# A two-layer hybrid attention block on one core: earlier-free memory under two sets of loads, another weave of LayerNorm rows, four groups in the second down phase

## The chip, the core and the metric

One of the eight cores of a Trainium2 chip runs the whole program. The metric is the device time of one execution in microseconds (us), smaller is better, over repeated executions. The engines are named as in the profile: PE (TensorE matmul) with PEld (its weight loads), DVE (VectorE), ACT (ScalarE), POOL (GpSimd), SP (SyncE, which here only issues DMA transfers). SPq and POOLq are the sequencers of SP and POOL, which issue transfers in program order.

## The reference, cut to what matters

Two layers over 1024 latent tokens (and 256 context tokens in layer 0), model width 1024, all in float32:

```python
for i in range(2):
    y, yc = mixer_i(h, hc)                       # attention, then @ w_out
    x = layer_norm(ALPHA * x + g1 * y, ln1_g, ln1_b)
    h = x * (1.0 + sc2) + sh2
    x = layer_norm(ALPHA * x + g2 * conv_ffn(h, w_up, conv_w, conv_b, w_down), ln2_g, ln2_b)
```

Layer 0 mixes by grouped-query and neighbourhood attention, layer 1 by multi-head latent attention (MLA, 16 heads). `conv_ffn` projects to 2 x 2816 features, convolves the gate half along the tokens, multiplies and projects back. In layer 0 the context tokens go through all of it too.

## The kernel before, in words

Every float32 product is made of three matmuls on split operands (`three`): a value is cast to a high part (`split_hi`, L404, mostly on ACT) and the rest goes to a low part (`split_lo`, L412, on DVE or POOL). So each block of weights and activations costs one cast and one subtraction before PE can use it.

The tokens stand in three chunks: 0 and 1 are 512 latent tokens each, 2 the 256 context tokens (layer 0 only). After attention, `layer_tail(l)` does the rest of a layer in these stages:

- **proj** (L1320 to L1341): y @ w_out in eight output blocks m, into `acc`. Layer 0 first reads y back from DRAM (`load_y`, L1288, tiles `yr`, stored as `y_scr` by the attention), and takes chunks 0 and 2 together, then chunk 1. `load_wo` (L1303) loads and splits one block of w_out (`ro`, then `foh`, `fol`). In layer 1 y is still in SBUF.
- **ln1 rows** (L1405): per 128 tokens a `normalise` (L1344: transposes `pta`, the sum `za`, its statistics), then eight `back_rows` (L1374: transposes `pba`, scaled into `tmpa`, split to `h`). For chunk 1 also 20 steps that make the operands P5, P6, P7, P4, P3. They are Python generators: each `next` emits a row, so the order of the calls sets the program order.
- **up phase** (`up_step`, L1459): products `pu` of a Strassen-Winograd scheme, seven products (P1 to P7) per pair of feature blocks, with weight conversions `wP` and, between, the convolution.
- **down phase** (`down_items`, `down_step`): the ten pairs of feature blocks are taken in `GROUPS` (L1612). A group passes all seven products; each product of a group writes four PSUM tiles (`pd_P`), and DVE adds each into its accumulators (`gated`, L1781, `acd<-pd_P`). The weights of a group are summed (L1208 to L1220) and split on DVE, POOL and ACT.
- the end of the layer: `last_down`, `ln2`, and after layer 0 `layer1_head` (w_in, rms, `rotate`, `up_kv`, `up_q`), which writes q, k, v of the MLA to DRAM. Then the first head is loaded (`prep1`, L2229, on POOL's queue) and attention of layer 1 runs.

Memory is in pools that share addresses over time: a tile may be written once the last users of what lay there are done, and the order in which tags are first used sets which addresses they get. `T` (`tail{l}`, tags c4, r, b) lies over memory of the attention before it; `AC` (`acc{l}`), `E` (`end{l}`), and the pools of the first head (`att1f`) lie over memory of the stage before. Outside attention a scheduler orders the instructions of each engine from the program order and the dependencies.

The caller, in short:

```python
for m in range(2):
    load_wo()
if l == 0:
    load_y(0); load_y(2); load_y(1)
run(proj((0, 2) if l == 0 else (0,)))
rows = itertools.chain(ln1(2), ln1(0)) if l == 0 else ln1(0)
for _ in proj((1,)):
    for _ in range(3 if l == 0 else 2):
        next(rows, None)
```

## Time and profile before

| | |
|---|---|
| median of 3 runs | 3521.74 us (3517.38 to 3532.01) |
| the profiled execution | 3522.96 us, span in the trace 3521.1 us |
| PE busy | 3291.1 us, 93% of the span |
| DVE, ACT, POOL busy | 70%, 50%, 42% of the span |
| mean granted clock of TensorE | 0.972 of full speed |
| layer 0's tail (proj to `layer1_head`) | about 807 to 2160 us |
| MLA attention | 2171 to 2701 us |
| layer 1's tail | 2704 to the end; its down phase 3249 to 3461 us |

A row of the timeline gives start, duration, engine, line, operation, output and inputs, and in brackets how long the engine was idle before it and what ended the idle time. Since PE is busy for all but some 230 us, the time of the kernel is read from the places where PE is idle or runs at a lower clock.

### The profile page before, as it was taken

How to read it: one execution, taken by the hardware profiler on the slowest of the kernel's cores; microseconds unless marked ns; L12 is line 12 of the kernel's file. 1: busy time of each engine (PE TensorE's matmuls, PEld its weight loads, DVE VectorE, ACT ScalarE, POOL GpSimd, SP SyncE). 2: the span in 40 equal slices, each digit the busy share in tenths (PEclk: the TensorE clock that was granted, in tenths of full speed). 3: DMA queues.
4: the chain of work that ended last, by engine and by line, in shares of the span. 5: the costliest groups of instructions: out<-in, count | busy, mean ns of one | idle time of the engine just before them, and what ended most of it. 6: DMA issues, size and time to landing. Idle time of an engine off the chain costs nothing.

```text
span 3521.1 us, 52490 instructions
## 1 busy us (share of the span) xinstructions
PE 3291.1 (93%) x18730; PEld 2834.5 (81%) x18730; DVE 2480.9 (70%) x3850; ACT 1755.3 (50%) x3335; POOL 1461.3 (42%) x1714
## 2 busy tenths in 40 slices
PE   7998899888889999999999998999999989999997
PEld 5987788877778888888877777999998768888786
DVE  6687687774698888686765534777776476777776
ACT  4222677774464444443335323777776354444342
POOL 4543688651200000035634522888885200000864
PEclk9999999999999999999999998999999999999998
DMA  6357511665345554263323457233333333334541
GB/s 217 114 186 223 134 44 31 159 182 166 126 154 156 168 169 157 76 230 120 99 65 102 132 211 228 50 83 76 72 77 88 117 105 102 111 99 144 191 135 72
DMA packets 385314, 455.05 MB, mean 129 GB/s; under 512 B 28500, under 2 KB 256764, under 8 KB 385052
## 3 DMA queue, kind: packets, MB, share of 16 engines
q1 hardware_dynamic: 371852, 425.08, 40.1%
q10 hardware_dynamic: 11424, 18.94, 1.5%
q0 software_dynamic: 1776, 7.67, 0.7%
q8 instruction: 148, 2.42, 0.3%
q14 instruction: 114, 0.93, 0.1%
HBM read 329.31 MB, written 122.22 MB: 128 GB/s over the span
## 4 chain that ended last, share of the span: by engine, by line
PE 42%; DVE 4%; POOL 3%; ACT 2%; issue 2%; DMA 2%; SPq 0%; POOLq 0%; ACTq 0%; DVEq 0%
PE pu L1459 10%; PE pd_P L1789 8%; PE psum L194 6%; PE psum L335 4%; PE psum L304 4%; PE pw L417 2%; PE psq L417 2%; PE pso L417 2%; PE px L1789 1%; PE pl L417 1%; PE psk L417 1%; PE psv L417 0%; POOL dr L1216 0%; DMA k<-kr_scr 0%; DMA dr<-in_l_w_down_dram 0%
## 5 line engine op out<-in xcount | busy, mean ns | idle before, releaser
L194 PE MATMUL psum<-k,q 96*128 96x512 f32 (+1 forms) x1152 | 273.1, 374 | 13.8 <-DMA k<-kr_scr 11.2
L412 POOL TENSOR_TENSOR dP<-dr,dP 128x512 fp32r<-128x512 f32 x40 | 56.1, 1421 | 487.6 <-ACT dP L404 465.1
L412 POOL TENSOR_TENSOR aal<-aa,aah 128x512 fp32r<-128x512 f32 x32 | 50.7, 1595 | 447.5 <-ACT aah L404 372.6
L194 PEld LDWEIGHTS psum<-k,q 96*128 96x128 f32 x1152 | 197.2, 193 | 42.4 <-issue 11.6
L264 POOL TENSOR_SCALAR p_m<-p_m,st_m 128x640 f32<-128x640 f32 x256 | 201.8, 801 | 12.6
L320 DVE TENSOR_TENSOR pl_m<-psum,ph_m 128x512 fp32r<-128x512 f32 x256 | 174.8, 684 | 37.4 <-ACT ph_m L314 36.4
L304 PE MATMUL psum<-ident,p_m 128*128 128x128 f32 x1280 | 193.3, 274 | 2.5 <-DVE pl_m L320 2.2
L251 ACT ACTIVATE p_m<-psum,st_m 128x1024 f32<-128x1024 f32 (+2 forms) x192 | 186.8, 983 | 17.0 <-DVE st_m L244 16.1
L314 ACT CAST ph_m<-psum 128x512 fp32r<-128x512 f32 x256 | 150.5, 589 | 88.7 <-PE psum L304 39.4
L552 DVE SCALAR_TENSOR_TENSOR aa<-aw,silu_late,aa 128x512 f32<-128x512 f32 x224 | 186.7, 862 | 8.1 <-DMA aw<-in_l_w_ada_dram 7.4
L335 PE MATMUL psum<-ph_m,v 128*128 128x256 f32 x640 | 175.3, 301 | 0.6 <-DVE y_m L353 0.6
L1781 DVE SCALAR_TENSOR_TENSOR acd<-pd_P,mods,acd 128x512 f32<-128x512 f32 x196 | 142.0, 742 | 44.8 <-PE pd_P L1789 44.6
L335 PE MATMUL psum<-ph,v 128*128 128x256 f32 (+1 forms) x512 | 150.4, 317 | 23.2 <-DVE y L368 12.1
L241 DVE TENSOR_REDUCE st_m<-psum 128x1 f32<-128x1024 f32 (+1 forms) x128 | 105.5, 824 | 88.1 <-PE psum L194 88.0
L320 DVE TENSOR_TENSOR pl<-psum,ph 128x512 fp32r<-128x512 f32 (+1 forms) x224 | 144.6, 647 | 31.1 <-ACT ph L314 28.0
L335 PE MATMUL psum<-pl_m,v 128*128 128x256 f32 x640 | 164.0, 282 | 0.0
L304 PE MATMUL psum<-ident,p 128*128 128x128 f32 x960 | 151.9, 278 | 10.4 <-ACT p_c L118 4.2
L264 POOL TENSOR_SCALAR p<-p,st 128x640 f32<-128x640 f32 x192 | 152.3, 801 | 12.6
L314 ACT CAST ph<-psum 128x512 fp32r<-128x512 f32 (+1 forms) x224 | 122.8, 557 | 67.5 <-PE psum L304 60.5
L304 PEld LDWEIGHTS psum<-ident,p_m 128*128 128x128 f32 x1280 | 149.0, 141 | 3.7 <-DVE pl_m L320 3.1
L304 PEld LDWEIGHTS psum<-ident,p 128*128 128x128 f32 x960 | 110.5, 142 | 28.9 <-DVE pl L320 8.2
L335 PE MATMUL psum<-pl,v 128*128 128x256 f32 (+1 forms) x512 | 132.5, 282 | 0.0
(605 smaller groups left out, 11283.4 us busy)
## 6 DMA issues: line engine op xcount, KB each, us to landing
aw<-in_l_w_ada_dram SPq DMA_DIRECT2D x96, 512.0 KB
ur<-in_l_w_up_dram SPq DMA_DIRECT2D x176, 256.0 KB
ar_P<-a_scr SPq DMA_DIRECT2D x140, 256.0 KB
a_scr<-a_t SPq DMA_DIRECT2D x80, 256.0 KB
dr<-in_l_w_down_dram SPq DMA_DIRECT2D x80, 256.0 KB
ro<-in_l_w_out_dram SPq DMA_DIRECT2D x64, 256.0 KB
a_scr<-cv SPq DMA_DIRECT2D x60, 256.0 KB
v<-v_scr SPq DMA_DIRECT2D x17, 640.0 KB
```

The costliest lines, as they stand in the source:

```text
L194: nc.tensor.matmul(u["s"][bank][:, c:e], q[:, qc], ks, start=pi == 0, stop=pi == len(u["passes"]) - 1)
L251: nc.scalar.activation(pt, src if bias is None else pt, AF.Exp, bias=st[:, j, 2:3], scale=1.0 if bias is None else -1.0, accum_out=st[:, j ...
L264: nc.gpsimd.tensor_scalar(pt, pt, st[:, j, 7:8], 0.0, op0=ALU.mult, op1=ALU.add)
L304: nc.tensor.transpose(tp[:, off + bi * P : off + bi * P + P], pts[j][:, c : c + P], ident)
L314: nc.scalar.copy(ph[:, :w], tp[:, :w])
L320: nc.vector.tensor_tensor(pl[:, :w], tps[g][:, :w], ph[:, :w].bitcast(F32), ALU.subtract)
L335: nc.tensor.matmul(u["av"][:, q0 : q0 + bw], u["v"][:, kt, :], m[:, off : off + bw], start=first and part == 0, stop=last and part == 1, s ...
L417: nc.tensor.matmul(ps, s, m, start=i == 0, stop=i == n - 1)
L552: nc.vector.scalar_tensor_tensor(accs[c], w, sck, accs[c], op0=ALU.mult, op1=ALU.add)
L1459: nc.tensor.matmul(ps, st, mv, start=start and i == 0, stop=i == len(pairs) - 1, skip_group_check=True)
L1781: nc.vector.scalar_tensor_tensor(acc[ci][:, m, :], src, mod(l, ci // 2, 5, m), acc[ci][:, m, :], op0=ALU.mult, op1=ALU.add)
L1789: nc.tensor.matmul(ps, st, mv, start=start and i == 0, stop=i == len(pairs) - 1, skip_group_check=True)
```

## The change

Five parts. (1) In layer 0 y is read in single blocks of 128x512 (24 loads) into tag `r`, in place of 12 loads of two blocks into tag `aw`; one block of w_out comes first, then y of chunks 0 and 2, the second block of w_out, y of chunk 1. Its first tiles are touched in another order, which puts `c4` ahead of `r` and `b` in `T`. For chunks 0 and 2 the first two output blocks take k = 0 to 6 first and k = 7, the last pair of heads, at the end. (2) The ln1 rows of chunks 2 and 0 are woven into `proj((1,))` by a written list of turns, and those of chunk 1 skip the first two up steps and then come by six (layer 0) or three (layer 1). (3) In `layer1_head` the small tiles go to `T` and the large ones stay in `AC`; the h1 tile of chunk 2 is the first in `E`; the last group of heads makes all of `up_kv(3)` ahead of most of `up_q(3)`. (4) In layer 1 the first block of w_out takes the same first-touched tiles. (5) Layer 1's down phase takes its pairs in four groups, 2 + 3 + 3 + 2, in place of three, 3 + 4 + 3. The matmuls are the same in number.

```diff
-            for g in range(4):
-                raw = tl("aw", (2, 512), f"yr{l}_{ci}_{g}")
...
+            for k in range(KB):
+                raw = tl("r", (512,), f"yr{l}_{ci}_{k}")[:, :cn]
+                nc.sync.dma_start(raw, y_scr[k * P : (k + 1) * P, c0 : c0 + cn])
+                split_hi(yh[:, k, :], raw, "act")
+                split_lo(yl[:, k, :], raw, yh[:, k, :], "dve")
...
+            early = 2 if l == 0 and cis[0] == 0 else 0
...
+                    if m < early:
+                        product(m, wh, wl, ci, range(KB - 1), ps)
+                        later.append((m, wh, wl, ci, ps))
...
+                if m == early - 1:
+                    for m_, wh, wl, ci, ps in later:
+                        product(m_, wh, wl, ci, range(KB - 1, KB), ps)
+                        evict(m_, ci, ps)
...
-        GROUPS = [(0, 1), (2, 3, 4), (5, 6, 7), (8, 9)] if l == 0 else [(0, 1, 2), (3, 4, 5, 6), (7, 8, 9)]
+        GROUPS = [(0, 1), (2, 3, 4), (5, 6, 7), (8, 9)]
...
-        for m in range(2):
-            load_wo()
+        wo.append(tuple(tl("fw", (KB, P), f"fo{s}{l}_first", F32R) for s in "hl"))
+        acc[0][:, 0, :]
+        load_wo()
         if l == 0:
             load_y(0)
             load_y(2)
+            load_wo()
             load_y(1)
...
+            x, c = ln1(0), ln1(2)
+            run(proj((0, 2)))
+            weave_in(
+                proj((1,)),
+                [(c, 2)], [(x, 2)], [(c, 3)], [(c, 3), (x, 1)], [(c, 2), (x, 1)], [(x, 2)], [(x, 3)], [(x, 3)],
+            )
...
+            weave_in(proj((1,)), [(x, 2)], [(x, 2)], [], [(x, 1)], [(x, 2)], [(x, 2)], [(x, 2)], [(x, 1)])
...
-            for _ in range(4 if l == 0 else 3):
+            for _ in range(0 if i < 2 else 6 if l == 0 else 3):
                 next(rows, None)
...
+        third = None
+        if l == 0:
+            third = block_tiles(tlE, "h10_2", chunks[2][1])
+            third[0][:, 0, :]
...
-        K = {"l": l, "T": AC if l == 0 else E, "tl": tl, "ps3": ps3, "ps1": ps1, "chunks": chunks,
+        K = {"l": l, "T": T if l == 0 else E, "AC": AC, "tl": tl, "ps3": ps3, "ps1": ps1, "chunks": chunks,
...
-            eh, el = (T.tile([P, 512], F32R, name=f"re{s}_{name}", tag="acc512", bufs=16)[:n] for s in "hl")
+            eh, el = (AC.tile([P, 512], F32R, name=f"re{s}_{name}", tag="acc512", bufs=16)[:n] for s in "hl")
...
-            weave(up_q(g), up_kv(g), "babababa" if g < 3 else "bbbabaa")
+            weave(up_q(g), up_kv(g), "babababa" if g < 3 else "bbbbaaa")
```

On SP's queue at the start of layer 0's proj (`ro` is w_out, `yr_<chunk>_<block>` is y) the order was, before:

```order
L1312 DMA ro_0_0_0_9489<-in_l_w_out_dram 128x4x128
L1312 DMA ro_0_0_1_9493<-in_l_w_out_dram 128x4x128
L1312 DMA ro_0_1_0_9499<-in_l_w_out_dram 128x4x128
L1312 DMA ro_0_1_1_9503<-in_l_w_out_dram 128x4x128
L1312 DMA ro_0_2_0_9621<-in_l_w_out_dram 128x4x128
L1312 DMA ro_0_2_1_9625<-in_l_w_out_dram 128x4x128
L1293 DMA yr_0_0_9507<-y_scr 128x2x512
L1293 DMA yr_0_1_9517<-y_scr 128x2x512
L1293 DMA yr_0_2_9527<-y_scr 128x2x512
L1293 DMA yr_0_3_9537<-y_scr 128x2x512
```

and is now:

```order
L1309 DMA ro_0_0_0_9490<-in_l_w_out_dram 128x4x128
L1309 DMA ro_0_0_1_9494<-in_l_w_out_dram 128x4x128
L1293 DMA yr_0_0_9498<-y_scr 128x512
L1293 DMA yr_0_1_9504<-y_scr 128x512
L1293 DMA yr_0_2_9510<-y_scr 128x512
L1293 DMA yr_0_3_9516<-y_scr 128x512
L1293 DMA yr_0_4_9522<-y_scr 128x512
L1293 DMA yr_0_5_9528<-y_scr 128x512
L1293 DMA yr_0_6_9534<-y_scr 128x512
L1293 DMA yr_0_7_9540<-y_scr 128x512
```

Four of the six transfers of w_out that stood ahead of y now stand behind it, and y comes in half-size pieces.

On DVE in layer 0's `proj((1,))` (`za_<chunk>_<j>` is a normalise, `tmpa_2` a back row of chunk 2, `fol` a low part of w_out) stood, after the statistics of `za_2_1`:

```order
L1367 TENSOR_SCALAR rs_a_2_1_10208<-mv_a_2_1_10206,rs_a_2_1_10208 128x1
L412 TENSOR_TENSOR fol_1_5_10366<-ro_1_5_1_10371,foh_1_5_10365 128x512
L1389 TENSOR_SCALAR tmpa_2_0_10216<-pba_2_0_10213,der_0_9478 128x256
L1389 TENSOR_SCALAR tmpa_2_1_10265<-pba_2_1_10262,der_0_9478 128x256
L412 TENSOR_TENSOR h_2l_10223<-tmpa_2_0_10216,h_2h_10221 128x256
L1389 TENSOR_SCALAR tmpa_2_2_10275<-pba_2_2_10272,der_0_9478 128x256
```

and now:

```order
L1385 TENSOR_SCALAR rs_a_2_1_10232<-mv_a_2_1_10230,rs_a_2_1_10232 128x1
L1376 SCALAR_TENSOR_TENSOR za_0_0_10276<-xk_0_10274,pta_0_0_0_10277 128x512
L1376 SCALAR_TENSOR_TENSOR za_0_0_10276<-xk_0_10274,pta_0_0_1_10283 128x512
L494 BN_STATS st_a_0_0_10289<-za_0_0_10276 128x6
L495 BN_STATS st_a_0_0_10289<-za_0_0_10276 128x6
L497 BN_AGGR mv_a_0_0_10292<-st_a_0_0_10289 128x2
```

The normalise of chunk 0 now stands between chunk 2's normalise and chunk 2's back rows, about one block of proj ahead of its own use.

On POOL at the start of layer 1's down phase (`aP2l`, `dP` low parts of activations and weights, `ds`, `dr` weight sums, the second number in `dP_1_<pair>` is the pair) stood:

```order
L412 TENSOR_TENSOR aP2l_0_32815<-ar_0_P_32726,aP2h_0_32814 128x512
L412 TENSOR_TENSOR aP2l_2_32823<-ar_2_P_32730,aP2h_2_32822 128x512
L1212 TENSOR_TENSOR ds_1_0_32912<-ds_1_0_32910,dr_0_00_32708 128x512
L1216 TENSOR_TENSOR dr_0_10_32732<-dr_0_00_32708,dr_0_10_32732 128x512
L1212 TENSOR_TENSOR ds_1_1_32919<-ds_1_1_32917,dr_1_00_32710 128x512
L1216 TENSOR_TENSOR dr_1_10_32736<-dr_1_00_32710,dr_1_10_32736 128x512
L1212 TENSOR_TENSOR ds_1_2_32926<-ds_1_2_32924,dr_2_00_32712 128x512
L1216 TENSOR_TENSOR dr_2_10_32740<-dr_2_00_32712,dr_2_10_32740 128x512
L412 TENSOR_TENSOR aP6l_0_32932<-ar_0_P_32744,aP6h_0_32931 128x512
L412 TENSOR_TENSOR dP_1_0_32914<-ds_1_0_32912,dP_1_0_32914 128x512
```

and now:

```order
L412 TENSOR_TENSOR aP2l_0_32813<-ar_0_P_32744,aP2h_0_32812 128x512
L1212 TENSOR_TENSOR ds_1_0_32892<-ds_1_0_32890,dr_0_00_32732 128x512
L412 TENSOR_TENSOR dP_1_0_32806<-dr_0_01_32740,dP_1_0_32806 128x512
L412 TENSOR_TENSOR dP_1_1_32809<-dr_1_01_32742,dP_1_1_32809 128x512
L1212 TENSOR_TENSOR ds_1_1_32899<-ds_1_1_32897,dr_1_00_32734 128x512
L1216 TENSOR_TENSOR dr_0_10_32748<-dr_0_00_32732,dr_0_10_32748 128x512
L412 TENSOR_TENSOR aP6l_0_32905<-ar_0_P_32756,aP6h_0_32904 128x512
L1216 TENSOR_TENSOR dr_1_10_32752<-dr_1_00_32734,dr_1_10_32752 128x512
L412 TENSOR_TENSOR aP5l_0_32964<-ar_0_P_32802,aP5h_0_32963 128x512
L412 TENSOR_TENSOR aP7l_0_33020<-ar_0_P_32886,aP7h_0_33019 128x512
L412 TENSOR_TENSOR dP_1_0_32894<-ds_1_0_32892,dP_1_0_32894 128x512
L412 TENSOR_TENSOR dP_1_1_32901<-ds_1_1_32899,dP_1_1_32901 128x512
```

Ahead of the first `dP` of P6 stood twelve operations (the three `dP` of P2 come before the rows shown); now there are ten, with the low parts of P5 and P7 of one pair among them.

## Rows read from the trace of the kernel before

**Rows 1.** The page's first section: busy time, share, instructions.

```profile
PE 3291.1 (93%) x18730; PEld 2834.5 (81%) x18730; DVE 2480.9 (70%) x3850; ACT 1755.3 (50%) x3335; POOL 1461.3 (42%) x1714
```

**Rows 2.** Stretches: start:end, length, busy of PE PEld DVE ACT POOL, PEclk, DMA share, GB/s.

```profile
796.00:888.00 92.00, 79.95 (x460) 68.75 (x460) 32.66 (x65) 39.68 (x78) 8.61 (x8) 0.94 0.52 159
888.00:1060.00 172.00, 151.50 (x773) 124.11 (x772) 136.52 (x230) 91.48 (x151) 25.38 (x25) 0.94 0.45 145
976.00:1004.00 28.00, 20.98 (x93) 16.27 (x92) 26.00 (x44) 19.21 (x35) 0.00 (x0) 0.81 0.33 110
2144.00:2184.00 40.00, 26.76 (x99) 21.51 (x98) 13.53 (x21) 10.38 (x20) 9.06 (x12) 0.76 0.89 249
2842.00:2892.00 50.00, 40.95 (x158) 32.18 (x159) 40.94 (x61) 25.27 (x42) 0.00 (x0) 0.91 0.32 100
3249.00:3310.00 61.00, 52.66 (x219) 42.25 (x218) 48.99 (x51) 28.27 (x50) 51.18 (x33) 0.92 0.69 241
3310.00:3461.00 151.00, 148.72 (x650) 122.79 (x648) 103.87 (x122) 50.41 (x91) 98.37 (x67) 0.99 0.35 112
1536.00:1575.00 39.00, 36.20 (x176) 30.89 (x175) 37.41 (x50) 16.85 (x29) 24.53 (x18) 0.96 0.72 240
```

**Rows 3.** Timeline, PE: start of layer 0's proj, its LayerNorm rows and up phase.

```profile
815.99 0.79 PE L417 MATMUL pso<-y_0h,foh 128*128 128x512 f32 x1 [8.77 <-ACT y_0h L404]
...
826.58 0.39 PE L417 MATMUL pso<-y_0h,foh 128*128 128x512 f32 x1
...
896.43 0.48 PE L1382 MATMUL pba<-ident,za 128*128 128x128 f32 x1 [4.12 <-DVE za L1370]
...
998.30 0.80 PE L1459 MATMUL pu<-h_P7h,wP 128*128 128x512 f32 x1 [6.54 <-ACT wP L404]
```

**Rows 4.** Start of layer 0's proj: SP's issues, the store of y, ACT's first cast.

```profile
804.69 3.15 SPq L1312 DMA_DIRECT2D ro<-in_l_w_out_dram  x6
807.95 16.23 SPq L1293 DMA_DIRECT2D yr<-y_scr  x12
...
L1082 POOL DMA_DIRECT2D y_scr<-y x1: 606/606/606, 808.4 to 808.4; - x1
...
815.32 0.62 ACT L404 CAST y_0h<-yr 128x512 fp32r<-128x512 f32 x1 [3.46 <-DMA yr<-y_scr]
```

**Rows 5.** First MLA head: POOL's timeline, transfers to landing (last column us), PE.

```profile
2148.15 2.85 POOL L2017 TENSOR_TENSOR qev<-qev,cosT 128x512 f32<-128x512 f32 x2 [30.11 <-DVE rel_q L412]
2151.66 0.70 POOL L2229 DMA_DIRECT2D q<-q_scr  x1 [0.65 <-POOL qev L2017]
...
2160.77 0.58 POOL L2229 DMA_DIRECT2D k<-k_scr  x1 [7.84 <-PE psq L417]
...
k<-kr_scr POOLq DMA_DIRECT2D x1, 320.0 KB, 9.9
...
2171.38 1.19 PE L194 MATMUL psum<-k,q 96*128 96x512 f32 x2 [11.17 <-DMA k<-kr_scr]
```

**Rows 6.** Layer 1: ACT's last cast of attention, PE's first proj, PE's waits 2760 to 2900.

```profile
2701.90 0.40 ACT L357 CAST y_1h<-y_m 64x256 fp32r<-64x256 f32 x1 [0.55 <-DVE y_m L353]
...
2704.68 0.80 PE L417 MATMUL pso<-y_0h,foh 128*128 128x512 f32 x1 [3.74 <-ACT foh L404]
...
PE pu L1459 <- ACT wP L404: 12.8, 3, 4.8
```

**Rows 7.** Down phases: PE's waits in layer 1, a wait in layer 0, the gated additions.

```profile
3281.89 0.79 PE L1789 MATMUL pd_P<-aP6l,dP 128*128 128x512 f32 x1 [7.64 <-POOL aP6l L412]
...
3348.92 0.80 PE L1789 MATMUL pd_P<-aP6l,dP 128*128 128x512 f32 x1 [2.28 <-POOL aP6l L412]
...
1550.35 7.38 PE L1789 MATMUL px<-cx,dP 128*128 128x256 f32 x48 [2.80 <-DVE acd L1781]
...
L1781 DVE SCALAR_TENSOR_TENSOR acd<-pd_P,mods,acd 128x512 f32<-128x512 f32 x196 | 142.0, 742 | 44.8 <-PE pd_P L1789 44.6
```

More of the change, by code (lines that the diff above doesn't have):

```diff
@@ L1307, in load_wo @@
                 return
-            wh, wl = (tl("fw", (KB, P), f"fo{s}{l}_{p}_{m}", F32R) for s in "hl")
+            first = p == 0 and m == 0
+            wh, wl = wo.pop() if first else (tl("fw", (KB, P), f"fo{s}{l}_{p}_{m}", F32R) for s in "hl")
             for half in range(2):
@@ L1320, in proj, with product, evict @@
         def proj(cis):
+            early = 2 if l == 0 and cis[0] == 0 else 0
+            later = []
+            def product(m, wh, wl, ci, ks, ps):
+                cn = chunks[ci][1]
+                yh, yl = ytiles[ci]
+                pairs = [p3 for k in ks for p3 in three(wh[:, k, :], wl[:, k, :], yh[:, k, :], yl[:, k, :])]
+                for i, (st, mv) in enumerate(pairs):
+                    nc.tensor.matmul(
+                        ps[:, :cn], st, mv, start=ks[0] == 0 and i == 0, stop=ks[-1] == KB - 1 and i == len(pairs) - 1,
+                        skip_group_check=True,
+                    )
+            def evict(m, ci, ps):
+                c0, cn = chunks[ci]
+                gate = mod(l, ci // 2, 2, m)
+                if l == 0:
+                    nc.scalar.activation(acc[ci][:, m, :], ps[:, :cn], AF.Copy, scale=gate)
+                else:
+                    xr = tl("xr", (512,), f"xr{l}_{ci}_{m}")
+                    nc.sync.dma_start(xr[:, :cn], x2_scr[m * P : (m + 1) * P, c0 : c0 + cn])
+                    nc.vector.scalar_tensor_tensor(
+                        acc[ci][:, m, :], ps[:, :cn], gate, xr[:, :cn], op0=ALU.mult, op1=ALU.add
+                    )
             for m in range(KB):
@@ L1725, in step, with weave_in @@
                     pending.pop(0)
-        for m in range(2):
-            load_wo()
+        def weave_in(products, *turns):
+            turns = iter(turns)
+            for _ in products:
+                for rows, n in next(turns, ()):
+                    for _ in range(n):
+                        next(rows, None)
+            for turn in turns:
+                for rows, n in turn:
+                    for _ in range(n):
+                        next(rows, None)
+        wo.append(tuple(tl("fw", (KB, P), f"fo{s}{l}_first", F32R) for s in "hl"))
+        acc[0][:, 0, :]
+        load_wo()
         if l == 0:
@@ L1731, in layer_tail @@
             load_y(2)
+            load_wo()
             load_y(1)
-        run(proj((0, 2) if l == 0 else (0,)))
-        rows = itertools.chain(ln1(2), ln1(0)) if l == 0 else ln1(0)
-        for _ in proj((1,)):
-            for _ in range(3 if l == 0 else 2):
-                next(rows, None)
-        run(rows)
+            x, c = ln1(0), ln1(2)
[3 more added lines that the diff above has]
+                [(c, 2)], [(x, 2)], [(c, 3)], [(c, 3), (x, 1)], [(c, 2), (x, 1)], [(x, 2)], [(x, 3)], [(x, 3)],
+            )
+            run(c)
+        else:
+            load_wo()
+            x = ln1(0)
+            run(proj((0,)))
+            weave_in(proj((1,)), [(x, 2)], [(x, 2)], [], [(x, 1)], [(x, 2)], [(x, 2)], [(x, 2)], [(x, 1)])
+        run(x)
         fill()
```

38 lines of the change are left out of this document (10 added, 28 removed).

## The prediction

> **What bounds the kernel now.** First the page: PE is busy 93% of the span and the next engine, DVE, 70% [rows 1]. So 230 us are idle on PE, and PE's work is the same in number after the change; all that the change can win is idle time of PE and time at the lower clock. Then the table of stretches [rows 2], for each place that the change touches: PE busy against the length gives the idle time there, PEclk tells what the clock took, and the DVE and POOL columns tell whether another engine is full. Last the timeline, for who ended each wait [rows 3 to 7]. In these six places PE waits for something made late by DVE, ACT, POOL or a transfer, mostly at the start of a stage. Of TensorE's two levels (1.2 and 2.4 GHz) the rows show the lower after such waits: a mean of 0.76 around the first MLA head, 0.94 in layer 0's LayerNorm stretch.
>
> **The change part by part.** The sum is made against the profiled execution, 3522.96 us, 1.2 us above the median of the three runs; 0.5% (17.6 us) is about what a measurement of this kernel can tell from no change.
>
> *A, start of layer 0's proj.* PE stops at 815.99 - 8.77 = 807.22 and starts proj at 815.99; the second output block begins at 826.58 [rows 3]. The six transfers of w_out are issued at 804.69 and y behind them; the last store of y is issued at 808.4, and ACT's first cast of y starts at 815.32 on a landing [rows 4]. In the built program the first w_out tile waits for a DVE read of the attention that lies some 6 us before 804.69, y's first five blocks wait for no engine, and only block 7 needs the last store, which the new product order puts last. So the first cast can come before 809, PE starts near 809.4, and the first blocks go at DVE's pace: one 512-column block needs three matmuls of 0.229 us at full clock (148.72 us for 650 in the down phase [rows 2]), and DVE one low part of about the same length as the three. I put the second output block at 821.6: **-5 us**. Bounds: -8.8, the whole wait; and +3: SP took 16.23 us for 12 loads, 1.35 each, and 16 loads (chunks 0 and 2) at that price from 806 end at 827.6 against 824.2, if the seven `r` slots pace them as the waits did before. I take the nearer to the gain because the loads that must be first have no wait. Doubling the y loads itself costs SP 12 more issues, beside other work.
>
> *B, LayerNorm rows in layer 0.* From 888 to 1060 PE is idle for 172 - 151.5 = 20.5 us, 4.12 at 896.43 (back row right behind its own normalise) and 6.54 at 998.30, and the clock takes 0.06 x 172 = 10.3 us [rows 2, 3]. The weave puts one block of proj (24 matmuls, 5.5 us) between normalise and back rows, so the 4.12 goes, and about a quarter of the clock's loss with it, 2.6. The small waits (20.5 - 4.12 - 6.54 = 9.8) I let go by 1.3 only, and the 6.54 not at all: there DVE is busy 26.0 of 28 us [rows 2], and moving rows takes no work from DVE. **-8 us**, between -16.5 (all small waits go too) and +3 (chunk 1's rows, which skip two up steps, come later than the weights did).
>
> *C, first MLA head.* PE ends `up_q` at 2171.38 - 11.17 = 2160.21. k waited 7.84 us on POOL for memory that the last `psq` held and was issued at 2160.77; k's second part landed 9.9 us after its issue [rows 5]. In the built program k and v wait for no engine, so they follow q, which follows the rotation on POOL (2148.15 to 2151.0). That puts k's second part at about 2152.9 and its landing at 2162.8: the wait shrinks from 11.2 to 2.6, -8.6, and I take 1.4 for the clock (0.24 x 40 = 9.6 us are lost to it around here [rows 2]). **-10 us**; bounds -17 and 0. The all-of-`up_kv(3)`-first weave costs nothing on PE, which has the same products; DVE is at 13.5 of 40 us there. [...]
>
> *D, start of layer 1.* ACT is free of attention at 2702.30, but PE starts at 2704.68 on a cast that waited for w_out [rows 6]. The transfers now wait for earlier DMA only, so a cast of 0.6 us can follow at once: PE at 2703.0, **-2 us** with rounding; bounds -3.74 and 0.
>
> *E, LayerNorm rows in layer 1.* PE waits 12.8 us for `wP` three times [rows 6]; DVE is at 40.9 of 50 us there, PEclk 0.91 [rows 2]. The weave and the later rows of chunk 1 change who comes first on DVE, not how much. **-4 us**; bounds -17 (12.8 and 0.09 x 50 of clock) and +4 (chunk 1's rows start two steps later and need six more operations in the way).
>
> *F, down phase of layer 1.* At its start PE waits 7.64 us for POOL, and 2.28 at the second group [rows 7]; POOL is busy 51.2 of 61 us with 33 operations, 1.55 each, DVE 49.0, PEclk 0.92 [rows 2]. With three pairs twelve POOL operations (18.6 us) stand ahead of P6's first weights, with two ten (15.5), while PE's products P1 and P2 shrink by a third (24 matmuls, 5.5 us, in place of 36, 8.2 us). So P6's wait becomes about 4 us in place of 8.3 with its small neighbour, the clock dip with it is worth 2 to 3 (0.08 x 61 = 4.9 lost now), the second group behaves like layer 0's, which is the same group. Against that stand 28 gated additions more (four per product and group, seven products), 28 x 0.742 = 20.8 us of DVE [rows 7]. From 3249 to 3461 DVE is busy 152.9 of 212 us, with them 173.7, or 82%: they fit beside PE on the whole. Only the first group is tight: 20.8 of gates, some 12 of splits, 8 of convolution left over and 6 for the next group are about 47 us against 40. **-6 us**; bounds -14 (waits and clock of both places) and +15 (all 20.8 on the path against the 6).
>
> The moves of small tiles between `T`, `AC` and `E` change addresses and waits, not operations; where a new wait fell on a path it would be in C's bounds.
>
> Sum: -5 - 8 - 10 - 2 - 4 - 6 = **-35 us**, 3522.96 - 35 = **3488 us**.
>
> **The rivals.**
> 1. *Transfers issued earlier land no earlier.* DMA share is already 0.89 around the first head [rows 2]; the slots of `r` or the stores of k and v pace the loads. A and C fall to 0 and -2, so that -22 is left: 3501. [...] Against it: k waited for memory, not for the queue. Chance 0.13.
> 2. *DVE sets the end of both up starts.* What is won at the weave is waited for at the next `wP`. DVE's 26.0 of 28 at 976 speaks for it, its 40.9 of 50 in layer 1 against. B and E go: 3500. Chance 0.15.
> 3. *Both, or only C and D halfway*: -8, 3515. Chance 0.15. That a part doesn't do what it says is in here: the scheduler, not the code, orders the engines, and a tile laid elsewhere may meet another late user.
> 4. *Slower: gates bound the down phase.* With two or three pairs a product gives each PSUM tile six or nine matmuls, 1.4 or 2.0 us, in which DVE has to do a gate of 0.74 and its splits. Layer 0's group of two shows DVE at 37.4 of 39 us and one PE wait of 2.80 on a gated addition [rows 2, 7]. If that wait came at each of the 28 product changes, 78 us would be lost: 3522.96 - 29 + 78 = 3572. It ends slower than before from 1.1 us per change. Against it: layer 0 has the context's gates on top, and shows it once. Chance 0.05.
>
> **How the numbers follow.** The sum has 0.52, with its own range from 3468 (B, C and E near their low bounds) to 3503. Rivals 1 and 2 lie about on the line of 0.5%, 3504, and a larger share of them below it. Faster by more than 0.5%: 0.52 and three quarters of 0.28, rounded 0.74; within 0.5%: 0.20; slower by more: 0.06. The range that holds 8 in 10 goes from 3466 to 3514.
>
> **What would show it.** A: the second output block's first matmul less than 15 us after attention's last one (19.4 now). B: no wait of several us on `pba<-ident,za`, the wait on `wP` at the up start still there. C: the first scores within 4 us of the last `psq`. D: the first `pso` of layer 1 within 1 us of ACT's last attention cast. F: the wait on `aP6l` under 5 us and no new wait of over 1 us on `acd`. It is wrong if PE's idle time falls by less than 18 us, or if new waits on `acd`, `yr` or `wP` take the place of those named.

## The result, and the profile after

| | before | after |
|---|---|---|
| median of 14 runs each, in turn on the same chips | 3523.03 us (3517.38 to 3532.01) | 3499.47 us (3496.03 to 3517.53) |
| ratio after / before | 1 | 0.9935, 95% interval 0.9924 to 0.9947 |
| the profiled execution's span | 3521.1 us | 3496.1 us |
| mean granted clock of TensorE | 0.972 | 0.978 |

The change is faster by 23.6 us (0.65%), on the side of the 0.5% that had the most chance, and 11.5 us short of the forecast's 3488. The page of after, its first section:

```profile
PE 3288.0 (94%) x18730; PEld 2825.1 (81%) x18730; DVE 2488.5 (71%) x3878; ACT 1756.7 (50%) x3335; POOL 1467.0 (42%) x1714
```

PE's matmuls are the same in number as in [rows 1]; its idle time fell from 3521.1 - 3291.1 = 230.0 to 208.1 us. DVE has 28 operations more, F's gates. The stretches that answer to [rows 2], moved with the work they cover:

```profile
796.00:888.00 92.00, 84.07 (x473) 71.38 (x472) 34.49 (x69) 40.62 (x78) 8.93 (x9) 0.96 0.54 159
886.00:1058.00 172.00, 154.71 (x782) 127.45 (x781) 135.76 (x231) 92.70 (x153) 25.82 (x25) 0.93 0.46 147
971.00:999.00 28.00, 19.16 (x68) 13.52 (x67) 25.10 (x42) 19.70 (x35) 0.00 (x0) 0.80 0.37 129
2134.00:2174.00 40.00, 33.92 (x137) 26.83 (x136) 17.08 (x24) 14.10 (x27) 15.21 (x21) 0.87 0.90 232
2815.00:2865.00 50.00, 39.71 (x144) 29.68 (x143) 39.37 (x60) 22.76 (x37) 0.00 (x0) 0.86 0.25 77
3226.00:3287.00 61.00, 54.37 (x237) 43.76 (x237) 46.65 (x57) 23.83 (x41) 45.27 (x31) 1.00 0.66 229
1532.00:1571.00 39.00, 39.00 (x196) 33.22 (x195) 36.70 (x47) 17.00 (x30) 28.54 (x19) 1.00 0.79 264
```

The two up starts (third and fifth row) are no better than before, the fifth has a lower clock (0.86 against 0.91). The first MLA head and both down phases are better, and the last row, in **layer 0's down phase**, has no idle time left; the prediction forecast nothing there.

Whole-span times vary between executions of the same code: the stretch up to the last product of layer 0's attention, where nothing was changed, took 804.1 to 815.0 us in the fourteen profiles of this study. So terms of a few us are read as distances between the start times of named matmuls on PE, in one profile of each kernel. The last column gives the spread over after and those kernels of the experiments whose code for the stretch is that of after:

| stretch on PE, start to start | before | after | difference | forecast | same code as after |
|---|---|---|---|---|---|
| last product of attention 0 to chunk 1's first proj product (A) | 77.88 | 75.71 | -2.2 | -5 | 74.9 to 76.0 |
| to P1 of layer 0's down phase (B) | 651.65 | 649.34 | -2.3 | -8 | 649.3 to 653.6 |
| to `last_down`'s first matmul (layer 0's down phase) | 261.01 | 252.71 | -8.3 | 0 | 252.7 to 254.2 |
| to the last `psq` of `layer1_head` | 362.34 | 364.55 | +2.2 | 0 | 361.6 to 365.1 |
| to the first MLA scores (C) | 11.56 | 3.79 | -7.8 | } -10 | 3.8 |
| to the last product of attention 1 | 529.28 | 527.61 | -1.7 | } | 526.3 to 529.5 |
| to the first proj product of layer 1 (D) | 4.02 | 2.33 | -1.7 | -2 | 2.3 |
| to P1 of its down phase (E) | 544.64 | 541.98 | -2.7 | -4 | 542.0 to 546.4 |
| to the closing transposes (F) | 222.79 | 221.29 | -1.5 | -6 | 220.5 to 222.9 |

With +0.9 ahead of A these add up to the -25.0 between the two spans, within rounding. The parts that were forecast bring -19.9 of -35; the remaining -5.2 are layer 0's down phase, less the +2.2 and the +0.9. Only in A, in layer 0's down phase, in C and in D does the value of before lie outside the spread of the last column. The differences in the other stretches, B, E and F among them, cannot be told from chance by these profiles.

### The profile page after: what moved, and what is told of

The parts are those of the page before. It is cut to its first block, busy times and chain, and to the rows that moved or that the text cites. A ratio compares the mean times of both kernels' runs of the same rounds, so it can differ in the third digit from the quotient of the medians.

```text
span 3496.1 us, 52574 instructions
## 1 busy us (share of the span) xinstructions
PE 3288.0 (94%) x18730; PEld 2825.1 (81%) x18730; DVE 2488.5 (71%) x3878; ACT 1756.7 (50%) x3335; POOL 1467.0 (42%) x1714
## 5 line engine op out<-in xcount | busy, mean ns | idle before, releaser
L412 POOL TENSOR_TENSOR aP2l<-ar_P,aP2h 128x512 fp32r<-128x512 f32 x10 | 14.5, 1454 | 566.7 <-ACT aP2h L404 438.2
L1825 DVE SCALAR_TENSOR_TENSOR acd<-pd_P,mods,acd 128x512 f32<-128x512 f32 x224 | 160.8, 741 | 36.0 <-PE pd_P L1833 27.1
L335 PE MATMUL psum<-ph,v 128*128 128x256 f32 (+1 forms) x512 | 150.2, 316 | 23.6 <-DVE y L368 12.4
```

What stands on the lines that cost most here:

```text
L335: nc.tensor.matmul(u["av"][:, q0 : q0 + bw], u["v"][:, kt, :], m[:, off : off + bw], start=first and part == 0, stop=last and part == 1, s ...
L412: e.tensor_tensor(dst, src, hi.bitcast(F32), ALU.subtract)
L1825: nc.vector.scalar_tensor_tensor(acc[ci][:, m, :], src, mod(l, ci // 2, 5, m), acc[ci][:, m, :], op0=ALU.mult, op1=ALU.add)
```

## The experiments

Each kernel is the changed one with one edit, unless it says otherwise. Ratios are to the kernel before, timed beside it on the same chip.

**1. Why layer 0's down phase gained.** The timeline of the kernel before, on DVE and (fourth row) POOL, ahead of the wait of 2.80 us on a gated addition in [rows 7]:

```profile
1539.11 1.27 DVE L1918 TENSOR_SCALAR der<-vec 128x8 f32<-128x8 f32 x1
1540.29 0.16 DVE L1919 TENSOR_SCALAR der<-vec 128x8 f32<-128x8 f32 x1
1540.37 1.26 DVE L1921 TENSOR_TENSOR der<-vec,mods 128x8 f32<-128x8 f32 x1
...
1540.31 2.55 POOL L412 TENSOR_TENSOR dP<-ds,dP 128x512 fp32r<-128x512 f32 x2
...
1544.14 0.74 DVE L1781 SCALAR_TENSOR_TENSOR acd<-pd_P,mods,acd 128x512 f32<-128x512 f32 x1
```

Eight tiny operations on `der2` (128x8 each) held DVE from 1539.11 to 1544.14, and the gated addition behind them was 5 us late. Every other one took 1.26 us, as long as one POOL operation beside it (2.55 / 2). In the changed kernel `der2` lies in `T`, free early, and the operations on it went to idle places, the first two to 809.5 and the other six to 1403.4; DVE in the trace of after:

```profile
809.51 0.30 DVE L1962 TENSOR_SCALAR der<-vec 128x8 f32<-128x8 f32 x1
...
1403.36 0.16 DVE L1965 TENSOR_TENSOR der<-vec,mods 128x8 f32<-128x8 f32 x1
...
1535.50 0.74 DVE L1825 SCALAR_TENSOR_TENSOR acd<-pd_P,mods,acd 128x512 f32<-128x512 f32 x1
```

The first kernel puts that tile alone back:

```diff
-        der = T.tile([P, 6, 8], F32, name="der2")
+        der = AC.tile([P, 6, 8], F32, name="der2")
```

> The changed kernel with the one small tile der2 put back where it was (pool AC in place of T); nothing else. Theory: eight tiny DVE operations on der2 stood in DVE's queue at the start of layer 0's down phase (1539 to 1544 us before), most of them 1.25 us long beside POOL, and made the gated additions late; with der2 in T they run at 809 us. Then this kernel has them back at the down phase, PE waits about 2.8 us for a gated addition ahead of the context's products again, and the stretch from the first product of the down phase to its last block is 5 to 9 us longer than the changed kernel's 252.7 us; the time rises by 4 to 9 us. Rival: that stretch is shorter for another reason (order of tiles in E, noise): it stays within 1.5 us of 252.7.

Measured: 3504.95 us, ratio 0.995 (0.9934 to 0.9966), and the stretch went from 252.71 to 258.73 us. DVE's queue and PE's wait came back, in its trace:

```profile
1544.62 1.26 DVE L1965 TENSOR_TENSOR der<-vec,mods 128x8 f32<-128x8 f32 x1
...
1554.61 7.50 PE L1833 MATMUL px<-cx,dP 128*128 128x256 f32 x48 [2.79 <-DVE acd L1825]
```

The 6.0 us between the two kernels are two things. The place of one tile of 48 columns is worth 4.5 us: the wait of 2.8 and the lower clock around it (granted clock 0.91 in the 20 us from 1545, against 1.00 in after). By the next wait on `acd`, at 1613.07 against 1600.66 in after, that 4.5 is complete (72.3 us behind P1, against 67.8). The other 1.5 us come 146 us later, where both kernels wait 2.2 us for a gated addition: the clock is 0.91 in the 20 us behind that wait in this kernel, and 1.00 in after. That one comes and goes: of the fourteen kernels six show 0.91 there, four of them with `der2` in `T`, such as the one without `third` of experiment 2 (first row; second row after; columns as in [rows 2]):

```profile
1746.00:1766.00 20.00, 17.87 (x95) 16.06 (x96) 13.65 (x22) 5.18 (x10) 6.93 (x7) 0.91 0.11 34
1744.60:1764.60 20.00, 17.87 (x101) 15.82 (x102) 14.30 (x23) 5.17 (x10) 8.39 (x8) 1.00 0.12 34
```

Those four took 254.2 us for the stretch, and seven others 252.7. The last 2.3 us of the 8.3 are a wait ahead of `last_down`'s first product, in the kernel before (first row) and in the one with layer 0's old weave (experiment 3, second row; 255.1 us), and in no other:

```profile
1797.48 0.47 PE L417 MATMUL pl<-lah,fh_d 128*128 128x512 f32 x1 [2.25 <-DVE acd L1781]
...
1787.26 0.47 PE L417 MATMUL pl<-lah,fh_d 128*128 128x512 f32 x1 [2.25 <-DVE acd L1821]
```

So of the 8.3 us 4.5 are the place of `der2`, 2.3 go with the weave of layer 0's rows, by a way that no run shows, and 1.5 are a lower clock that after was spared and others were not.

**2. What brought C.** Two kernels: one without the early reservation of `third` in `E`, and one with the old weave in the last group of heads.

```diff
             third = block_tiles(tlE, "h10_2", chunks[2][1])
-            third[0][:, 0, :]
```

> The changed kernel without the early first touch of chunk 2's h1 tile, so that pool E is laid out as before (c4 under b). Theory: it is this order of E alone that freed the first MLA head's memory; without it q and k wait again for the last products of up_q, and PE waits 10 to 12 us between up_q's last matmul and the first scores (3.8 in the changed kernel), the time rises by 6 to 9 us. Rival: the small tiles' moves or the weave of the last heads did it: the gap stays below 6 us.

```diff
-            weave(up_q(g), up_kv(g), "babababa" if g < 3 else "bbbbaaa")
+            weave(up_q(g), up_kv(g), "babababa" if g < 3 else "bbbabaa")
```

> The changed kernel with the last weave of the heads as before (bbbabaa). Theory: it has no part in the first head's gain: the gap from up_q's last product to the first scores stays at 3.8 us. The stretch from layer 0's last feature blocks to up_q's end became 2 us longer with the change (362.3 to 364.3; 361.8 with pool E laid out as before): if that is the weave's, it is 362 to 363 here; if it is E's order, it stays at 364.

Without the reservation 3508.66 us, ratio 0.9956 (0.9939 to 0.9973), and C is as long as before: 11.24 us between last `psq` and first scores. Its trace, POOL's issue and PE:

```profile
2151.17 0.58 POOL L2272 DMA_DIRECT2D k<-k_scr  x1 [7.96 <-PE psq L417]
...
2161.45 4.80 PE L194 MATMUL psum<-k,q 96*128 96x512 f32 x12 [10.84 <-DMA k<-kr_scr]
```

With the old weave 3502.45 us (one run) and 3.83 us: the weave has no part in C. Its stretch to the last `psq` took 363.73 us, inside the spread of the kernels with the new weave, so it does not tell where the +2.2 of that stretch comes from. The order in which `E`'s tags are first used decides the wait: without the reservation it is back, though the small tiles still lie in `T`. Whether the reservation would be enough without their move was not run. What ends the wait in after, in its timeline (POOL, ACT, PE):

```profile
2140.17 0.54 POOL L2273 DMA_DIRECT2D k<-kr_scr  x1
...
2150.55 0.59 ACT L404 CAST qev_0h<-psq 128x512 fp32r<-128x512 f32 x1 [3.52 <-PE psq L417]
2151.16 1.28 ACT L377 ACT_TABLE_LOAD   x1
...
2152.56 0.57 ACT L404 CAST qev_512h<-psq 128x512 fp32r<-128x512 f32 x1
...
2153.91 0.50 PE L194 MATMUL psum<-k,q 96*128 96x512 f32 x1 [3.39 <-DVE qev_512l L412]
```

and in its list of transfers, whose last column is the time from issue to landing:

```profile
k<-kr_scr POOLq DMA_DIRECT2D x1, 320.0 KB, 9.5
```

The loads went straight behind q, and k's second part had landed by 2140.17 + 9.5 = 2149.7, ahead of the last `psq`'s end (2150.52). Now the eviction of that `psq` is last, with the table load of an early exponential (L377) between its two casts.

**3. The weave of LayerNorm rows.** Layer 0's weave as before, layer 1's as before, and one repair of layer 0's:

```diff
-            x, c = ln1(0), ln1(2)
             run(proj((0, 2)))
-            weave_in(
-                proj((1,)),
-                [(c, 2)], [(x, 2)], [(c, 3)], [(c, 3), (x, 1)], [(c, 2), (x, 1)], [(x, 2)], [(x, 3)], [(x, 3)],
-            )
-            run(c)
+            x = itertools.chain(ln1(2), ln1(0))
+            weave_in(proj((1,)), *[[(x, 3)]] * 8)
...
-            for _ in range(0 if i < 2 else 6 if l == 0 else 3):
+            for _ in range(4 if l == 0 else 0 if i < 2 else 3):
```

> The changed kernel with layer 0's LayerNorm rows woven as before (three steps per block, chunk 2 then chunk 0; chunk 1 four steps per up step from the first). Theory: the new weave takes the wait at the first back row away and puts one of 4.9 us in its place, on chunk 0's last normalise, which waits for its row of x from DRAM; so it is worth 2 to 4 us: from the first product of chunk 1 to the first product of the down phase 651 to 654 us against 649.3. Rival: it is worth the 8 us that were forecast: 657. Rival: nothing: 648.5 to 650.

```diff
-            weave_in(proj((1,)), [(x, 2)], [(x, 2)], [], [(x, 1)], [(x, 2)], [(x, 2)], [(x, 2)], [(x, 1)])
+            weave_in(proj((1,)), *[[(x, 2)]] * 8)
...
-            for _ in range(0 if i < 2 else 6 if l == 0 else 3):
+            for _ in range(3 if l else 0 if i < 2 else 6):
```

> The changed kernel with layer 1's LayerNorm rows as before (two steps per block; chunk 1's from the first up step, three each). Theory: the new weave saves some 6 us inside proj and the up start gives nearly all of it back, because the weight conversions on ACT and DVE end at the same time; from the first product of proj to the first of the down phase it is 542 to 547 us as in the changed kernel (542.0, 542.5, 545.8, 546.4, 542.6 so far, 544.6 before). Rival: the weave is worth the 4 us that were forecast: 547 or more, with the longer part inside proj (101 us in place of 95.5). Rival: it costs: 541 or less.

With layer 0's undone: 3503.07 us, ratio 0.994 (0.9922 to 0.9958); B 650.51 against 649.34, within the spread of the kernels with the new weave (649.3 to 653.6 in the table). With layer 1's undone: 3499.64 us, 0.9939 (0.9920 to 0.9959); E 545.57 against 541.98. Neither ratio can be told from after's. E has two outcomes among kernels whose layer 1 is the same, 542.0 to 543.1 us (after and six others) and 546.0 and 546.4 (two, the one with layer 0's weave undone among them), and the 544.64 of the kernel before lies between them. The granted clock in the 50 us from the last `pso` is 0.93 in after and 0.89 in both of the longer ones, but 0.90 in two of the shorter, so it does not part them; what does is open. So layer 1's weave is worth between 0 and 3.6 us. The waits that took the places of the old ones, in the timeline of after (layer 0: PE, SP, DVE; then layer 1: DVE, PE):

```profile
932.01 0.69 PE L1400 MATMUL pba<-ident,za 128*128 128x128 f32 x2 [4.87 <-ACT za L1386]
...
977.98 0.79 PE L1477 MATMUL pu<-h_P5h,wP 128*128 128x512 f32 x1 [3.27 <-ACT h_P5h L404]
...
995.56 0.80 PE L1551 MATMUL px<-h_2h,wP 128*128 128x256 f32 x2 [3.48 <-DVE wP L412]
1000.34 0.79 PE L1477 MATMUL pu<-h_P6h,wP 128*128 128x512 f32 x1 [2.27 <-ACT wP L404]
...
920.49 0.45 SPq L1431 DMA_DIRECT2D xk<-in_x_dram  x1
...
925.93 1.28 DVE L1376 SCALAR_TENSOR_TENSOR za<-xk,pta 128x512 f32<-128x512 f32 x2 [3.34 <-DMA xk<-in_x_dram]
...
2777.16 0.75 DVE L1340 SCALAR_TENSOR_TENSOR acc<-pso,mods,xr 128x512 f32<-128x512 f32 x1 [2.78 <-DMA xr<-x_scr]
...
2784.05 2.29 PE L1369 MATMUL pta<-ident,acc 128*128 128x128 f32 x19 [2.50 <-DVE acc L1340]
...
2832.73 0.80 PE L1477 MATMUL pu<-h_P6h,wP 128*128 128x512 f32 x1 [4.89 <-ACT wP L404]
```

In layer 0 the old wait of 4.12 [rows 3] is gone, and a wait of 4.87 stands at the last normalise of chunk 0, whose x row was issued at 920.49, just ahead of its need. The waits at the up start (3.27, 3.48, 2.27) add up to more than the 6.54 that stood there. In layer 1 proj lost its bubbles (last `pso` 95.45 us after the first, 101.79 before), and the evictions and `wP` took back 3.7 of the 6.3. The repair takes chunk 0's third and fourth normalise one block earlier:

```diff
-                [(c, 2)], [(x, 2)], [(c, 3)], [(c, 3), (x, 1)], [(c, 2), (x, 1)], [(x, 2)], [(x, 3)], [(x, 3)],
+                [(c, 2)], [(x, 2)], [(c, 3), (x, 1)], [(c, 3), (x, 1)], [(c, 2)], [(x, 2)], [(x, 3)], [(x, 3)],
```

> The changed kernel with the third and fourth normalise of chunk 0 in layer 0 each one block of proj earlier. Theory: PE's wait of 4.9 us on chunk 0's last normalise (932 us) comes from its row of x, loaded late into a slot that proj's weights held; one block earlier it goes, and the first product of the down phase comes 2 to 5 us sooner (from chunk 1's first product 645 to 647.5 us against 649.3). Rival: the weight conversions of the up start (DVE full at 980 to 1000) set the end: the wait goes and the waits behind it grow, 648.5 to 650.5.

Measured: 3494.27 us, ratio 0.9918 (0.9902 to 0.9934). The 4.87 is gone, proj's last `pso` starts 54.41 us after chunk 1's first (61.58 in after), and of these 7.2 us the up phase gives back 5.2: B is 647.34, below all kernels without the repair; the two of experiment 6 that have it too take 646.3 and 645.8. By the time alone it cannot be told from after, as the two intervals overlap. The waits on DVE and ACT at the up start stay, 2.95, 3.48 and 2.28 us.

**4. The start of layer 0's proj.** In after PE waits 2.04 us for the first cast, as forecast, but the second cast is late (SP's issues, ACT, PE):

```profile
800.63 18.16 SPq L1293 DMA_DIRECT2D yr<-y_scr  x16
...
809.47 0.61 ACT L404 CAST y_0h<-yr 128x512 fp32r<-128x512 f32 x1
813.02 3.74 ACT L404 CAST y_0h<-yr 128x512 fp32r<-128x512 f32 x7 [2.94 <-DMA y_scr<-y]
...
810.13 0.56 PE L1327 MATMUL pso<-y_0h,foh_first 128*128 128x512 f32 x1 [2.04 <-ACT y_0h L404]
...
823.20 0.39 PE L1327 MATMUL pso<-y_0h,foh 128*128 128x512 f32 x1
...
832.63 0.50 PE L1327 MATMUL pso<-y_0h,foh 128*128 128x512 f32 x1 [0.93 <-ACT foh L404]
```

The high tile of y's block 1 lies on the last attention output, which the last store still reads; so not block 7's load alone waits for that store. Three kernels. The first asks for the tiles of blocks 7 and 1 in the other order:

```diff
             yh, yl = ytiles[ci]
+            for k in (0, 7, 2, 3, 4, 5, 6, 1) if ci == 0 else ():
+                yh[:, k, :], yl[:, k, :]
```

> The changed kernel with the tiles of y's blocks 1 and 7 (chunk 0) swapped in memory. Theory: in the changed kernel ACT's second cast of y waits from 810.1 to 813.0 us for the last store of y, because the tile it writes lies on the attention output that this store reads, and everything behind it on ACT waits too; block 7 needs that store anyway. Swapped, the seven first casts follow each other, PE's gaps of 1.0 and 0.8 us go and the lower clock ends earlier: the first product of chunk 1 comes 2 to 4 us earlier (71 us or less after attention's last product on PE, against 75.5). Rival: the seven slots of the loads and the transfers set the pace: chunk 1 begins within 1 us of where it does now.

3497.99 us, ratio 0.9933 (0.991 to 0.9957). The edit moved no tile, since addresses follow the first writes, and the cast waited 2.95 us for the same store: it tells nothing of the theory. The second has POOL split blocks 1 and 2, and PE take them last:

```diff
-                split_hi(yh[:, k, :], raw, "act")
-                split_lo(yl[:, k, :], raw, yh[:, k, :], "dve")
+                eng = ci == 0 and k in (1, 2)
+                split_hi(yh[:, k, :], raw, "pool" if eng else "act")
+                split_lo(yl[:, k, :], raw, yh[:, k, :], "pool" if eng else "dve")
...
-                        product(m, wh, wl, ci, range(KB - 1), ps)
+                        product(m, wh, wl, ci, (0, 3, 4, 5, 6), ps)
...
-                        product(m_, wh, wl, ci, range(KB - 1, KB), ps)
+                        product(m_, wh, wl, ci, (1, 2, 7), ps)
```

> The changed kernel with blocks 1 and 2 of y (chunk 0) split on POOL in place of ACT and DVE, and multiplied with block 7 at the end in the first two output blocks. The earlier swap of names (i_y) did not move any tile: addresses follow the order of first writes, and the second tile written lies on the attention's last output whichever block it holds, so the second cast still waited 2.95 us for the store. Theory: that wait held ACT; with the two blocks on POOL, ACT casts blocks 0, 3, 4 without a wait, PE's gaps of 1.0 and 0.8 us go, and chunk 1's first product comes 72 to 74.5 us after attention's last product on PE (75.4 to 76.0 so far). Rival: the loads' slots and landings set the pace, or POOL's slower splits come too late: 75 to 78.

3504.8 us, ratio 0.9949 (0.9934 to 0.9964), and A is longer, 78.03 us, at the upper end of what the rival expected. ACT's casts no longer wait for the store, and wait for loads in its place:

```profile
803.87 20.48 SPq L1293 DMA_DIRECT2D yr<-y_scr  x16
...
812.71 1.65 ACT L404 CAST y_0h<-yr 128x512 fp32r<-128x512 f32 x3
816.88 1.27 ACT L404 CAST y_0h<-yr 128x512 fp32r<-128x512 f32 x2 [2.52 <-DMA yr<-y_scr]
```

The sixteen loads go through seven slots of `r`, and a slot is free when its block is split. POOL began to split only at 816.47, behind the same store, and so held two slots longer; SP's issues stretched from 18.16 to 20.48 us. So POOL's lateness took the place of the wait that was removed, and what the store's wait costs A stays open. The third undoes the new loads and the product that is put off and issues both blocks of w_out ahead of y again, with the order in which tiles are first used left as it is after:

```diff
-            for k in range(KB):
-                raw = tl("r", (512,), f"yr{l}_{ci}_{k}")[:, :cn]
+            for g in range(4):
+                raw = tl("aw", (2, 512), f"yr{l}_{ci}_{g}")
...
-            early = 2 if l == 0 and cis[0] == 0 else 0
+            early = 0
...
+            load_wo()
             load_y(0)
             load_y(2)
-            load_wo()
             load_y(1)
```

> The changed kernel with y's loads as before (twelve, two blocks each, tag aw), both blocks of w_out ahead of them and the first two output blocks whole; the order in which tags are first touched stays. Theory: what the start gained (77.9 us to 75.3 to 76.0 from attention's last product to chunk 1's first) is from these loads and the late block, so it is 77.5 to 80 again. Rival: the order of the tags alone, which lets w_out load 5 us earlier, did it: 75 to 76.5 or less.

3500.4 us, ratio 0.9928 (0.9912 to 0.9945), A 76.81 us, between what the two views expected: the loads and the order of products are worth about 1 us, as much as the order of first use.

**5. Layer 1's groups.**

```diff
-        GROUPS = [(0, 1), (2, 3, 4), (5, 6, 7), (8, 9)]
+        GROUPS = [(0, 1), (2, 3, 4), (5, 6, 7), (8, 9)] if l == 0 else [(0, 1, 2), (3, 4, 5, 6), (7, 8, 9)]
```

> The changed kernel with layer 1's down phase back in three groups (3 + 4 + 3). Theory: the four groups are worth little, 1 to 3 us, because what POOL no longer delays, ACT's casts, DVE's low parts and gated additions now do (waits of 3.6, 2.3, 1.9, 1.2, 1.6 us in the changed kernel): the stretch from the first product of layer 1's down phase to the first transpose of its end is 222 to 225 us against 221.3. Rival one: they are worth the 6 us that were forecast and something else hid it: 227 or more. Rival two: they cost, since 28 gated additions more lie on DVE: 220 or less.

3501.36 us, ratio 0.9939 (0.9923 to 0.9954); F 223.22 us, where all kernels with four groups took 220.5 to 222.9. So the groups are worth 0.3 to 2.7 us. PE's waits in after's down phase, as the waits view lists them (total, times, longest):

```profile
PE pd_P L1833 <- ACT dP L404: 3.6, 1, 3.6
PE pd_P L1833 <- DVE acd L1825: 3.4, 3, 1.6
PE pd_P L1833 <- DVE dP L412: 2.3, 1, 2.3
PE pd_P L1833 <- POOL aP6l L412: 1.9, 1, 1.9
PE pl L417 <- DVE acd L1825: 0.9, 1, 0.9
```

POOL's 9.9 us (7.64 and 2.28 [rows 7]) shrank to 1.9, and 10.2 us for ACT and DVE stand in their place; with three groups that view lists no such wait on ACT or DVE, in the kernel before or in this one. What is left of the gain is the clock in the 61 us from the start: 0.92 in both kernels with three groups, 1.00 in after and 0.94 to 1.00 in the others with four.

**6. Together, to beat both.** One kernel joins the repair of experiment 3, chunk 2's y loads in pairs of blocks through the tag `aw` (so that chunk 0 has the slots of `r`), layer 1's x rows fetched two outputs ahead, and no early exponential before the MLA attention (its table load stood in C's path). The second is the same with the early exponential.

```diff
+            if ci == 2:
+                for g in range(4):
+                    raw = tl("aw", (2, 512), f"yr{l}_{ci}_{g}")
...
+            if l == 1:
+                fetch(0, cis[0])
+                fetch(1, cis[0])
...
-                    xr = tl("xr", (512,), f"xr{l}_{ci}_{m}")
-                    nc.sync.dma_start(xr[:, :cn], x2_scr[m * P : (m + 1) * P, c0 : c0 + cn])
+                    if m + 2 < KB:
+                        fetch(m + 2, ci)
+                    xr = ahead.pop((m, ci))
...
-        attention(tc, pa, pp, ident, mone, units)
+        attention(tc, pa, pp, ident, mone, units, ahead=False)
```

> The changed kernel with four more edits, each in a stretch of its own: chunk 0's third and fourth normalise one block earlier (the edit measured as i_x); y of chunk 2 loaded in pairs of blocks into tag aw, outside the seven slots of r; in layer 1 the rows of x for the residual asked for two blocks ahead; and no early exponential before the MLA attention, whose table load stood between the last two evictions of up_q on ACT. Theory, by what each waits for now: the seven slots pace the start (72 to 74.5 us from attention's last product to chunk 1's first, 75.3 to 76 now); the transfer of x's rows holds the last block of layer 1's proj (proj to the first product of the down phase 2 to 3 us shorter than 542 to 546); the table load costs 1.3 us between up_q and the scores (2.3 to 2.6 in place of 3.8, unless the load then falls on the first exponential). All of it with i_x: 6 to 9 us under the changed kernel, 3490 to 3494. Rivals, stretch by stretch: the store of y, not the slots, paces the start: 75 to 76.5; the weight conversions end the up start whatever proj does: 542 to 547; the table load shows up again in the first softmax: scores to the end of attention 1.3 us longer.

> The fastest version so far without its one part that seems to have cost time: the early ACT operation before the MLA attention is back, the normalise order of chunk 0, the paired y loads of chunk 2 and the x rows fetched two outputs ahead in layer 1 stay. Theory (the early operation's table load costs 0.65 us of the wait before the first scores and saves the wait on the first exponentials): the stretch from the first scores to the attention's last product goes from 532.5 back to about 527.6, the gap before the first scores from 3.1 to 3.8, the other stretches stay as they were (74.0 at the start of proj, 646.3 for the LayerNorm and up stretch of layer 0, 539 in layer 1); time 3486 to 3490 us, about 12 us below the changed kernel. Rival (the 5 us in the attention were chance, like the differences there between other runs, and the early operation costs what it delays): the attention stretch stays above 531 and the time is 3490 to 3494.

The first: 3491.31 us, ratio 0.9899 (0.9883 to 0.9915). A 74.03, B 646.3, E 539.25 us: each below after, so slots are part of what paces A (some 1 to 2 us), and the late x rows are 2.7 us of E. The attention behind C grew from 527.61 to 532.54. PE's waits there, and the stretch of the first 20 us, its columns those of [rows 2]:

```profile
2148.06 6.77 PE L194 MATMUL psum<-k,q 96*128 96x512 f32 x18 [2.74 <-DVE qev_512l L413]
2158.18 6.75 PE L194 MATMUL psum<-k,q 96*128 96x512 f32 x18 [3.34 <-ACT p_m L251]
```

```profile
2148.00:2168.00 20.00, 15.91 (x52) 12.73 (x53) 6.92 (x10) 6.85 (x14) 6.28 (x9) 0.58 1.08 268
```

The second: 3487.36 us (3481.12 to 3489.61), ratio 0.9900 (0.9884 to 0.9915); A 74.08, B 645.8, E 539.18, and the attention 527.78 us. The same places:

```profile
2144.31 5.10 PE L194 MATMUL psum<-k,q 96*128 96x512 f32 x18 [3.39 <-DVE qev_512l L412]
2151.48 6.05 PE L194 MATMUL psum<-k,q 96*128 96x512 f32 x18 [2.06 <-ACT p_m L251]
```

```profile
2144.30:2164.30 20.00, 17.08 (x72) 13.71 (x73) 9.63 (x12) 7.98 (x16) 9.65 (x15) 0.74 1.07 271
```

The table load out of the first wait (0.65 us shorter) is found again in the second (1.28 longer), and the lower clock lasts longer. So the two profiles show about 4 us for the early exponential, as attention in all other kernels took 526.3 to 529.5; the times do not: the two ratios are equal, as the kernel before took 3525.58 beside the first and 3522.38 beside the second. Both beat the changed kernel: their intervals lie below its 0.9924, by some 12 us at the middle.

## Why the prediction was right and wrong

**What bounds the kernel**: right. PE's idle time fell by 22 us and the span by 25; the rest is clock.

**A, -5, came to -2.2.** Attention's last product ends at 810.13 - 2.04 = 808.09, and the second output block starts 823.20 - 808.09 = 15.1 us later, against 19.36 before: 4.25 us sooner, and just over the 15 that was named. All of the first block, its k = 7 too, is done by then. Two steps failed. "y's first five blocks wait for no engine" overlooked that the second block's high tile waits for the last store. And the gain was measured at the second output block's start, as if it stayed to the end of the stage: 2.1 us of it went in the blocks behind, 1.1 in the second, most of it the 0.93 at 832.63 on w_out's third block, which SP issued from 827.54, behind all 24 y loads.

**B, -8, came to -2.3.** The 4.12 went, as said, but the 2.3 are within the spread of kernels with the same code. That no other wait would come was wrong: the same blocks' distance put a normalise ahead of its x row (4.87), the repair shows it, and the repair shows too that the up start takes back most of what proj wins. Rival 2 told this: DVE and the conversions set the up start, at 25.1 of 28 us busy.

**C, -10, came to -7.8.** Right in place, and near in size; the -1.7 in the attention behind it, where the forecast's 1.4 for the clock would lie, is within the spread of that stretch. The step on the reason was half right: the loads follow q, and k no longer ends the wait at all. k's second part lands before the last `psq` ends, not 2.6 us after, because q itself was issued 12.2 us before that end (8.6 before); what remains is the eviction. Rival 1 was wrong here: landing took 9.5 us, 9.9 before.

**D, -2, came to -1.7**, on the cast that was named (no experiment undid it; all kernels with the change show 2.3 us); the trace of after, PE:

```profile
2683.85 0.50 PE L1327 MATMUL pso<-y_0h,foh_first 128*128 128x512 f32 x1 [2.05 <-ACT foh_first L404]
```

**E, -4, came to -2.7**, which the two outcomes of E leave open. Proj won 6.3, and the evictions that wait for x rows and `wP` gave 3.7 back: rival 2 again, with a part (the x rows, 2.7 us) that is no engine's but a late fetch's.

**F, -6, came to -1.5**, and experiment 5 gives 0.3 to 2.7. P6's wait is 1.93, below the 4 forecast. The step that failed is that P6's wait was all there was: behind POOL stood ACT's and DVE's operands, at 3.63 and 2.33 us. Rival 4 was wrong: with 28 more gates the waits on `acd` are 4.3 us in all, the longest 1.61, not 2.80 at each change of product.

**"The moves of small tiles change addresses and waits, not operations"** is the largest error: layer 0's down phase gained 8.3 us, forecast at nothing, and experiment 1 shows 4.5 of it as the move of `der2`. The row was there ([rows 7], the 2.80 on `acd`), and rival 4 used it as a price of gates; what stood in DVE's queue ahead of that gate was not looked at.

**Its own signs.** C and D came as named, and PE's idle time fell by 21.9 us, more than the 18. A missed by 0.1 us. B missed (4.87 on `pba<-ident,za`), and F half (1.93 on `aP6l`, but 1.6 on `acd`). The last sign, new waits on `acd` or `wP` in the place of the old ones, came true in part: 3.48 us on `wP` in B, 3.4 us in all on `acd` in F. That the time is as near the forecast as it is owes something to luck: B, E and F gave little, and layer 0's down phase, forecast at nothing, made up for some of it. The chance of faster, 0.52 and three quarters of 0.28, adds up to 0.73, not 0.74.

Rival 2's 3500 is nearly the time measured, but by chance: B and E fell as it says, and A and F fell short too; layer 0's down phase made up for them.

## What to carry to other kernels

A wait on an engine's result is priced by what stands ahead of that result in the engine's queue: read it before calling the wait a price of the operation. Memory that is free earlier moves its users earlier too, small ones included, and an order of first use can be worth more than the transfers that it was made for. What is won at one wait is only kept if the next operand is early; name the next one, and measure the gain at the end of the stage. And before a difference of 2 or 3 us is given a cause, look how far kernels with the same code lie apart there.
